# Six instead of four units start early in a seven-product gate/up stage, in pairs, with operand sums spread out

## The chip, the core and the metric

The kernel runs on one core of one Trainium2 chip. The metric is the device time of one execution in microseconds (us), median of several runs. Times inside a run come from a trace of one profiled execution; they count from the first instruction of that execution.

Names of engines: PE is TensorE (matmuls and transposes), DVE is VectorE, ACT is ScalarE, POOL is GpSimd, SP is SyncE, which issues the DMAs. PSUM is the memory that PE writes; this kernel divides it into eight banks of 128x512 fp32, five called `L` and three called `M`.

## The reference, cut to what matters

One decoder block over 1024 tokens of width 1024: an RMSNorm, an input projection, a state-space mixer beside a retention mixer, an output projection, and then the part that the change touches:

```
h = rmsnorm(x, norm2_w[i])
a = jax.nn.silu(jnp.einsum("bsd,df->bsf", h, w_gate[i]))
u = jnp.einsum("bsd,df->bsf", h, w_up[i])
x = x + jnp.einsum("bsf,fd->bsd", a * u, w_down[i])
```

followed by a last RMSNorm. D_FF is 2816, so `w_gate` and `w_up` are 1024x2816 each.

## The kernel before

**Numbers and halves.** Every fp32 operand of a large matmul is split into a high and a low part (`split`: ACT copies with rounding, DVE subtracts), and each product is three matmuls (high x high, high x low, low x high). The 1024 tokens are handled as two halves of 512, called h = 0 and h = 1.

**A list of steps sets the order.** `steps` is a list of (block, k). `run_all` walks it: it first prepares operands up to three steps ahead (`advance`: DMA issue, then `split`), then emits the matmuls of the step, then calls the functions hooked to that step with `at(i, f)`. PE runs in exactly this order. The other engines' orders come out of a scheduler that takes the code in this order with some priorities; on each engine instructions then run strictly one after the other.

**The gate/up stage.** It is computed with a 2x2x2 scheme of seven products instead of eight: weight columns in two halves of 128, the model dimension in two halves, tokens in two halves. A `Unit` is 256 columns of `w_gate` or `w_up`; there are 22, alternating gate and up. Each product of a unit is one step: 12 matmuls of 128x512. Products 1 and 2 need only the token half h = 0 (operands `B[1]`, `B[2]`, the normed and transposed half h = 0). Products 3 to 7 need sums of both halves. Products that start a sum take the PSUM banks by turns, five `L` banks, then three `M` banks. Product 2 adds into the PSUM bank of product 1, so between the two ACT must copy the result of product 1 out of that bank (line 166, into the tile `ktok`).

**What happens before the other products can run.** The token half h = 1 (tiles `x0` to `x3`) becomes final only at the end of the output projection. Then `scale` (lines 333 to 342) multiplies its four 128x1024 tiles by the norm's factors on DVE. For each of four k, `b_sums(k)` (lines 869 to 892) has PE transpose two 128x512 pieces into two `M` banks (a **lot** of eight transposes, line 163), and then DVE and ACT form the sums in place and split them: line 884 (ACT) and lines 886, 887, 890 (DVE), with splits at lines 195 (ACT) and 196 (DVE). The names in these instructions: `M` the two banks, called t2 and t1 in the code, `u` the scaled copy of t2, `m0` to `m15` the split operands, `h0` to `h2` and `S` the sums F. With three `M` banks, the second bank of a lot is the one that held t1 of the lot before, free once DVE has split t1 (line 196); the first bank held t2 of the lot before the last, free after line 890. `b_rest(k)` splits the two halves of F for products 7 and 4.

**Order at the start of the stage.** Four units run products 1 and 2 first, one unit after the other (eight steps), and the `b_sums` of the four k are hooked to the steps 2, 3, 4 and 5 of these, all `b_rest` to step 6. Then the same four units run products 6, 5, 7, 3, 4, and the other 18 units run all seven in the order 1, 6, 5, 2, 7, 3, 4. In the first part the weights come as single 256 KB loads; from product 6 of the first unit on, as two 512 KB tiles per unit into `x0`, `x1` or `x2`, `x3` (line 936), which become free when the last lot of transposes has read them. Operands of products lie in a ring of seven slots (`wp` three, `x4` to `x7`).

**After products.** `use` (lines 1003 to 1020) applies tanh (line 1010, ACT), multiplies (lines 1011 and 1019, DVE) and stores.

Of the kernel before, what the change touches and what calls it, by code (L numbers as in the profile page):

```python
# [9 lines left out]
F32 = mybir.dt.float32  # L10
F32R = mybir.dt.float32r
I32 = mybir.dt.int32
AF = mybir.ActivationFunctionType
ALU = mybir.AluOpType
# [3 lines left out]
P = 128  # L18
DM = 1024
SEQ = 1024  # L20
TH = 512
# [44 lines left out]
def block_kernel(ctx: ExitStack, tc: tile.TileContext, x, norm1_w, w_in, conv_w, conv_b,  # L66
# [12 lines left out]
    def T(shape, tag, dt=F32, bufs=1):  # L79
        uid[0] += 1  # L80
        return sb.tile(list(shape), dt, tag=tag, name=f"{tag}_{uid[0]}", bufs=bufs)

    def bank(tag):
        uid[0] += 1
        return psum.tile([P, 512], F32, tag=tag, name=f"{tag}_{uid[0]}", bufs={"L": 5, "M": 3}[tag])
# [4 lines left out]
    tt, stt, ts = nc.vector.tensor_tensor, nc.vector.scalar_tensor_tensor, nc.vector.tensor_scalar  # L90
    act = nc.scalar.activation
# [70 lines left out]
    def tr(o, a):  # L162
        tc.keep_in_program_order(nc.tensor.transpose(o, a, ident))  # L163
# [4 lines left out]
    def rsqrt(dst, src, scale, eps, n):  # L168

        w = T([P, 3, 16], "nw", bufs=3)  # L170
        v, t, i = w[:, 0, :n], w[:, 1, :n], w[:, 2, :n]
        ts(v, src, scale, eps, op0=ALU.mult, op1=ALU.add)
        ts(i.bitcast(I32), v.bitcast(I32), 1, None, op0=ALU.logical_shift_right)
        ts(dst.bitcast(I32), i.bitcast(I32), -1.0, 1597463007.0, op0=ALU.mult, op1=ALU.add)
        ts(v, v, -0.5, None, op0=ALU.mult)
        for _ in range(3):
            tt(t, dst, v, op=ALU.mult)
            tt(t, t, dst, op=ALU.mult)
            stt(dst, t, 1.5, dst, op0=ALU.add, op1=ALU.mult)
# [13 lines left out]
    def split(pair, src):  # L193

        a = act(pair[:, 0], src, AF.Copy).ins  # L195
        d = tt(pair[:, 1], src, pair[:, 0].bitcast(F32), op=ALU.subtract).ins  # L196
        return a, d
# [7 lines left out]
    steps = []  # L205
# [3 lines left out]
    def at(i, f):  # L209
        hooks.setdefault(i, []).append(f)  # L210
# [119 lines left out]
    def norm_pieces(get, wcol, tags, res, also=None):  # L330


        st = {}

        def scale():
            xt, ssq = get()
            rs = T([P, NT], "rs", bufs=2)
            tt(rs, ssq[:, :, 0], ssq[:, :, 1], op=ALU.add)
            rsqrt(rs, rs, 1.0 / DM, EPS, NT)
            for t in range(NT):  # L340
                ts(xt[t], xt[t], rs[:, t:t + 1], None, op0=ALU.mult)
            st["x"] = xt

        def one(k):
            def f():
                b = bank("M")
                for t in range(NT):
                    tr(b[:, t * P:(t + 1) * P], st["x"][t][:, k * P:(k + 1) * P])
                if also and k < 4:
                    if k == 0:  # L350
                        st["qk"] = T([P, 4, 2, TH], "qk", F32R)
                    hp = st["qk"][:, k]
                else:
                    hp = T([P, 2, TH], tags[k], F32R)
                w = cols[:, wcol + k:wcol + k + 1]
                act(hp[:, 0, :], b, AF.Copy, scale=w)
                stt(hp[:, 1, :], b, w, hp[:, 0, :].bitcast(F32), op0=ALU.mult, op1=ALU.subtract)
                res.append(hp)
                if also:
                    also(k)(b, w)  # L360
            return f
        return scale, [one(k) for k in range(8)]

    def load_x(h):
# [493 lines left out]

    B = {4: [], 7: [], "F": []}

    def b_first(k):

        def f(b, w):
            if k < 4:
                B["F"].append(T([P, 2, TH], f"h{k}" if k < 3 else "S"))
            act(B["F"][k % 4][:, k // 4, :], b, AF.Copy, scale=w)
        return f

    def b_sums(k):

        def f():
            if k == 0:
                for i in (5, 6, 7, 3):
                    o = {5: 0, 6: 4, 7: 8, 3: 12}[i]
                    B[i] = [T([P, 2, TH], f"m{q}", F32R) for q in range(o, o + 4)]
            bs = []
            for q in (k + 4, k):
                b = bank("M")
                for t in range(NT):
                    tr(b[:, t * P:(t + 1) * P], H[1]["x2"][t][:, q * P:(q + 1) * P])  # L880
                bs.append(b)
            t2, t1 = bs
            b22 = T([P, TH], "u", bufs=2)
            act(b22, bs[0], AF.Copy, scale=cols[:, 12 + k:13 + k])
            F = B["F"][k]
            stt(t1, bs[1], cols[:, 8 + k:9 + k], F[:, 0], op0=ALU.mult, op1=ALU.subtract)
            tt(t2, b22, t1, op=ALU.subtract)
            split(B[6][k], t2)
            split(B[5][k], t1)
            tt(F, F, t2.unsqueeze(1).to_broadcast([P, 2, TH]), op=ALU.subtract)  # L890
            split(B[3][k], b22)
        return f

    def b_rest(k):
        def f():
            split(B[7][k], B["F"][k][:, 0])
            B[4].append(T([P, 2, TH], f"h{(k + 3) % 4}", F32R))
            split(B[4][k], B["F"][k][:, 1])
        return f

    slots = [("wp", 3), ("x4", 1), ("wp", 3), ("x5", 1), ("wp", 3), ("x6", 1), ("x7", 1)]
    nslot = [0]
    units = [0]
    stage = {}

    def slot():
        tag, n = slots[nslot[0] % 7]
        nslot[0] += 1
        return T([P, 2, 4, P], tag, F32R, bufs=n)

    class Unit:
# [4 lines left out]

        def __init__(self, w, c0, st, use, prods=ORDER):
            self.w, self.c0, self.st, self.use, self.prods = w, c0, st, use, prods
            self.first = len(steps)
            steps.extend((self, k) for k in range(len(prods)))  # L920
            self.last = len(steps) - 1
            self.K = len(prods)
            self.op = {}

        def load(self, k):
# [58 lines left out]
    def gate_up():  # L984
        def temp():
            return T([P, TH], "wr", bufs=5)

        ss = []

        def c1(n):  # L990
            if n == 0:
                stage["c1"] = T([P, 4, TH], "ktok")
                b = T([P, 3, 4, P], "kcB")
                stage["s2"] = b[:, 2]
                stage["c15"] = b.rearrange("p k j q -> p k (j q)")
                a = T([P, 2, TH], "wb0")
                ss.extend((a[:, 0], a[:, 1]))
            return stage["c1"][:, n % 4]

        def pair_of(b):  # L1000
            def gate(q, ps, add):
                if len(ss) == 2 and q:
                    a = T([P, 2, TH], "S")
                    ss.extend((a[:, 0], a[:, 1]))
                g = ps
                if add is not None:
                    g = temp()
                    tt(g, ps, add, op=ALU.add)
                t = temp()
                act(t, g, AF.Tanh, scale=0.5)  # L1010
                stt(ss[q], t, 1.0, g, op0=ALU.add, op1=ALU.mult)

            def up(q, ps, add):
                u = ps
                if add is not None:
                    u = temp()
                    tt(u, ps, add, op=ALU.add)
                a = T([P, TH], "u", bufs=2)
                stt(a, u, 0.5, ss[q], op0=ALU.mult, op1=ALU.mult)  # L1019
                nc.sync.dma_start(aD[q % 2][2 * b + q // 2], a)  # L1020
            return gate, up

        class St(dict):
            def __missing__(self, k):
                assert k == "c1"
                self[k] = c1(self.n)
                return self[k]
        us, todo, n = [], [], 0
        for b in range(NF // 2):
            for w, use in zip((w_gate, w_up), pair_of(b)):  # L1030
                st = St()
                st.n = n
                n += 1
                todo.append((w, 256 * b, st, use))
        EARLY = 4
        us += [Unit(*a, (1, 2)) for a in todo[:EARLY]]
        us += [Unit(*a, (6, 5, 7, 3, 4)) for a in todo[:EARLY]]
        us += [Unit(*a) for a in todo[EARLY:]]
        return us

    def down_block(h, b):
        d = H[h]
# [79 lines left out]
    for h in range(2):  # L1122
        H[h]["O"] = list(out_blocks(h))
    GU = gate_up()
    for h in range(2):
        H[h]["D"] = [down_block(h, b) for b in range(2)]
# [81 lines left out]
    s0 = I0["z0"].first  # L1208
# [12 lines left out]
    scale, ks = norm_pieces(lambda: got["x"], 0, HT, H[1]["hT"])  # L1221
# [6 lines left out]
    scale, ks = [None] * 2, [None] * 2  # L1228
# [3 lines left out]
    s0 = H[1]["O"][0].first  # L1232
# [3 lines left out]

    def b_ready():
        B[1], B[2] = hT2[:4], hT2[4:]
    s0 = GU[0].first
    at(s0 - 1, b_ready)  # L1240
    at(s0 - 1, scale[1])
    for k in range(4):
        at(s0 + 2 + k, b_sums(k))
        at(s0 + 6, b_rest(k))

    def load_final():
        wbf.append(T([P, DM], "wb0"))
# [30 lines left out]
```

## Time and profile before

| | us |
|---|---|
| median of 3 runs | 1528.23 (1526.89 to 1529.42) |
| the profiled execution, its own time | 1528.46 |
| span of its trace, first to last instruction | 1526.7 |
| PE busy in the span | 1496.4 |
| DVE busy | 1018.6 |
| ACT busy | 625.2 |

The page gives, for each engine, busy time and share; 40 slices of the span with the busy share in tenths; the chain of work that ended last (here 92% PE); and groups of instructions by line with mean duration and the idle time in front of them. Matmuls are pipelined: one is listed with some 395 ns, but the next one starts after some 233 ns, so starts, not durations, tell the rate. The mean granted clock of TensorE over the span is 0.994 of full speed. Finer questions go to the trace: a list of who waited for whom, and a timeline of one engine in a stretch, where `[0.69 <-ACT ktok L166]` behind an entry says that the engine stood idle for 0.69 us before it and what ended that.

### The profile page before, as it was taken

What the parts mean: (1) busy time and instruction counts of PE and PEld (TensorE: products, weight loads), DVE (VectorE), ACT (ScalarE), POOL (GpSimd) and SP (SyncE); (2) the same over time, 40 slices, a digit from 0 to 9 for tenths busy, and PEclk for the clock granted to TensorE, in tenths of its full rate; (3) what the DMA queues carried; (4) which work ended last, traced back from release to release, by engine and by line L of the source; (5) the groups of instructions that cost most, each with busy time, mean ns of one, the idle gap of its engine ahead of it and who ended that gap; (6) DMA issues with size and microseconds to landing.
All of it is one profiled execution on the core that took longest, in us unless ns stands there. A gap on an engine that the chain in (4) does not pass through costs nothing.

```text
span 1526.7 us, 20790 instructions
## 1 busy us (share of the span) xinstructions
PE 1496.4 (98%) x7408; PEld 1222.3 (80%) x7408; DVE 1018.6 (67%) x2175; ACT 625.2 (41%) x1219; POOL 33.2 (2%) x67
## 2 busy tenths in 40 slices
PE   6999999999999999999999899999999999999997
PEld 5888878887889878878887688888888887788886
DVE  4587788767688896578746976666666665346345
ACT  5344457444354655333444522222222234344232
POOL 1011000000000000000000000000000000000000
PEclk8999999999999999999999999999999999999999
DMA  7433466473425567645533332222222238455331
GB/s 195 137 92 98 116 203 190 121 242 105 130 77 148 167 204 248 214 146 175 187 118 97 97 111 78 81 83 83 76 83 83 83 105 293 133 176 188 126 112 68
DMA packets 139369, 208.68 MB, mean 137 GB/s; under 512 B 11172, under 2 KB 69376, under 8 KB 139264
## 3 DMA queue, kind: packets, MB, share of 16 engines
q1 hardware_dynamic: 138096, 205.90, 43.6%
q0 software_dynamic: 432, 0.59, 0.6%
q8 instruction: 58, 0.95, 0.3%
q10 hardware_dynamic: 736, 0.86, 0.2%
q14 instruction: 47, 0.39, 0.1%
HBM read 166.34 MB, written 40.96 MB: 136 GB/s over the span
## 4 chain that ended last, share of the span: by engine, by line
PE 92%; DMA 4%; DVE 2%; ACT 1%; issue 1%; SPq 0%; ACTq 0%; DVEq 0%
PE L L160 74%; PE M L160 16%; PE M L163 2%; DMA m<-aD 1%; DMA wr<-in_w_in_dram 1%; DMA wr<-in_w_down_dram 1%; DVE m L196 0%; DMA x<-in_w_gate_dram 0%; DMA kc<-in_consts_dram 0%; DMA ktok<-aD 0%; ACT m L195 0%; DMA m<-mixD 0%; DVE wp L249 0%; DVE u L1019 0%; ACT wp L248 0%
## 5 line engine op out<-in xcount | busy, mean ns | idle before, releaser
L249 DVE TENSOR_TENSOR wp<-wr,wp 128x512 fp32r<-128x512 f32 (+2 forms) x328 | 217.7, 665 | 224.3 <-ACT wp L248 223.1
L160 PE MATMUL L<-wp,m 128*128 128x512 f32 x1512 | 357.3, 395 | 1.5 <-DVE wp L249 0.9
L248 ACT ACTIVATE wp<-wr 128x512 fp32r<-128x512 f32 (+2 forms) x328 | 199.6, 610 | 361.8 <-PE L L160 294.9
L160 PEld LDWEIGHTS L<-wp,m 128*128 128x128 f32 x1512 | 282.0, 188 | 68.7 <-DVE wp L249 2.4
L160 PE MATMUL L<-wp,h 128*128 128x512 f32 (+2 forms) x1248 | 260.0, 365 | 0.0
L160 PEld LDWEIGHTS L<-wp,h 128*128 128x128 f32 x1248 | 215.4, 188 | 30.6 <-issue 5.1
L160 PE MATMUL L<-h,wp 128*128 128x512 f32 x972 | 234.1, 398 | 0.7 <-ACT ktok L166 0.7
L160 PEld LDWEIGHTS L<-h,wp 128*128 128x128 f32 x972 | 180.6, 188 | 44.5 <-ACT ktok L166 1.1
L160 PE MATMUL L<-m,x 128*128 128x512 f32 x336 | 82.7, 395 | 1.6 <-ACT x L195 1.2
L160 PE MATMUL L<-h,x 128*128 128x512 f32 x336 | 83.3, 396 | 0.7 <-ACT ktok L166 0.7
L160 PE MATMUL L<-m,wp 128*128 128x512 f32 x312 | 77.1, 395 | 0.0
L160 PEld LDWEIGHTS L<-m,x 128*128 128x128 f32 x336 | 62.9, 188 | 17.2 <-ACT x L195 1.6
L160 PEld LDWEIGHTS L<-h,x 128*128 128x128 f32 x336 | 62.9, 188 | 16.3 <-ACT ktok L166 1.1
L160 PEld LDWEIGHTS L<-m,wp 128*128 128x128 f32 x312 | 58.5, 187 | 14.4
L195 ACT ACTIVATE wp<-wr 128x512 fp32r<-128x512 f32 x46 | 29.0, 630 | 66.6 <-DVE wr L948 57.5
L195 ACT ACTIVATE x<-x 128x512 fp32r<-128x512 f32 x40 | 24.9, 623 | 72.5 <-PE M L160 32.4
L389 DVE SCALAR_TENSOR_TENSOR m<-m,cols,m 128x512 f32<-128x512 f32 x72 | 52.1, 745 | 3.6 <-ACT m L387 3.4
L160 PE MATMUL M<-m,wp 128*128 128x512 f32 x216 | 53.4, 395 | 0.0
L160 PEld LDWEIGHTS M<-m,wp 128*128 128x128 f32 x216 | 40.5, 188 | 9.9
L160 PE MATMUL M<-m,x 128*128 128x512 f32 x192 | 47.1, 394 | 0.0
L196 DVE TENSOR_TENSOR m<-m 128x512 fp32r<-128x512 f32 x32 | 21.8, 690 | 35.5 <-ACT m L195 35.5
L160 PE MATMUL M<-h,x 128*128 128x512 f32 x180 | 44.5, 395 | 0.0
(280 smaller groups left out, 1952.4 us busy)
## 6 DMA issues: line engine op xcount, KB each, us to landing
wr<-in_w_in_dram SPq DMA_DIRECT2D x144, 256.0 KB, 2.8
wr<-in_w_down_dram SPq DMA_DIRECT2D x88, 256.0 KB, 2.9
wr<-in_w_out_dram SPq DMA_DIRECT2D x64, 256.0 KB, 2.9
aD<-u SPq DMA_DIRECT2D x44, 256.0 KB, 2.0
x<-in_w_gate_dram SPq DMA_DIRECT2D x22, 512.0 KB, 3.9
x<-in_w_up_dram SPq DMA_DIRECT2D x22, 512.0 KB, 3.9
x<-in_x_dram SPq DMA_DIRECT2D x16, 512.0 KB, 4.1
m<-rD SPq DMA_DIRECT2D x16, 512.0 KB, 4.1
```

The costliest lines, as they stand in the source:

```text
L160: tc.keep_in_program_order(nc.tensor.matmul(o, a, b, start=start, stop=stop, **kw))
L163: tc.keep_in_program_order(nc.tensor.transpose(o, a, ident))
L195: a = act(pair[:, 0], src, AF.Copy).ins
L196: d = tt(pair[:, 1], src, pair[:, 0].bitcast(F32), op=ALU.subtract).ins
L248: newest["act"] = act(pair[:, 0, :n], raw[:, :n], AF.Copy).ins
L249: newest["dve"] = tt(pair[:, 1, :n], raw[:, :n], pair[:, 0, :n].bitcast(F32), op=ALU.subtract).ins
L389: stt(dst, u[:, q:q + TH], w[q], dst, op0=ALU.mult, op1=ALU.add)
```

## The change

1. Six units instead of four run products 1 and 2 early, and they go in pairs: product 1 of both, then product 2 of both (12 steps). Six units then run 6, 5, 7, 3, 4; the other 16 run all seven.
2. `b_sums` is hooked to steps 2, 4, 6, 8 of the stage (before 2, 3, 4, 5), `b_rest` to steps 9 and 10 (before 6).
3. In `b_sums` the split of `b22` (operand of product 3) moves up: its ACT part right behind line 884, its DVE part ahead of the other splits.
4. The copies of product 1 need six places (before four); the two new ones take `x7`, so that the ring of operand slots has six slots.
5. `scale` of the second norm puts tiles 1 and 3 on ACT and leaves 0 and 2 on DVE, in both token halves.

```diff
             for t in range(NT):
-                ts(xt[t], xt[t], rs[:, t:t + 1], None, op0=ALU.mult)
+                if wcol and t % 2:
+                    act(xt[t], xt[t], AF.Copy, scale=rs[:, t:t + 1])
+                else:
+                    ts(xt[t], xt[t], rs[:, t:t + 1], None, op0=ALU.mult)
...
             act(b22, bs[0], AF.Copy, scale=cols[:, 12 + k:13 + k])
+            act(B[3][k][:, 0], b22, AF.Copy)
             F = B["F"][k]
             stt(t1, bs[1], cols[:, 8 + k:9 + k], F[:, 0], op0=ALU.mult, op1=ALU.subtract)
             tt(t2, b22, t1, op=ALU.subtract)
+            tt(B[3][k][:, 1], b22, B[3][k][:, 0].bitcast(F32), op=ALU.subtract)
             split(B[6][k], t2)
             split(B[5][k], t1)
             tt(F, F, t2.unsqueeze(1).to_broadcast([P, 2, TH]), op=ALU.subtract)
-            split(B[3][k], b22)
...
-    slots = [("wp", 3), ("x4", 1), ("wp", 3), ("x5", 1), ("wp", 3), ("x6", 1), ("x7", 1)]
+    slots = [("wp", 3), ("x4", 1), ("wp", 3), ("x5", 1), ("wp", 3), ("x6", 1)]
...
-                stage["c1"] = T([P, 4, TH], "ktok")
+                a, c = T([P, 4, TH], "ktok"), T([P, 2, TH], "x7")
+                stage["c1"] = [a[:, q] for q in range(4)] + [c[:, q] for q in range(2)]
...
-        EARLY = 4
-        us += [Unit(*a, (1, 2)) for a in todo[:EARLY]]
-        us += [Unit(*a, (6, 5, 7, 3, 4)) for a in todo[:EARLY]]
-        us += [Unit(*a) for a in todo[EARLY:]]
-        return us
+        EARLY = 6
+        first = len(steps)
+
+        for i in range(0, EARLY, 2):
+            us = [Unit(*a, (1, 2)) for a in todo[i:i + 2]]
+            steps.extend((u, k) for k in range(2) for u in us)
+        for i, a in enumerate(todo):
+            u = Unit(*a, (6, 5, 7, 3, 4) if i < EARLY else Unit.ORDER)
+            steps.extend((u, k) for k in range(len(u.prods)))
+        return first
...
-        at(s0 + 2 + k, b_sums(k))
-        at(s0 + 6, b_rest(k))
+        at(s0 + 2 + 2 * k, b_sums(k))
+        at(s0 + 9 + k // 2, b_rest(k))
```

What stands where, first on PE at the start of the stage. `L_1282` is the PSUM bank of the first unit, `qk` and `h4` to `h7` the token half h = 0 (for products 1 and 2), `wp`, `x4`, `x5` the weights' operands, `M_` lines the transposes. Before:

```order
L160 MATMUL L_1282_8078<-qk_1195_7545,wp_1271_8005 128x512 x12
L160 MATMUL L_1282_8078<-h4_1231_7752,x4_1273_8022 128x512 x3
L160 MATMUL L_1282_8078<-h5_1237_7799,x4_1273_8022 128x512 x3
L160 MATMUL L_1282_8078<-h6_1247_7846,x4_1273_8022 128x512 x3
L160 MATMUL L_1282_8078<-h7_1253_7893,x4_1273_8022 128x512 x3
L160 MATMUL L_1291_8120<-qk_1195_7545,wp_1281_8075 128x512 x12
L163 MATMUL M_1308_8150<-kc_1_63,x0_1146_7275 128x128
```

After:

```order
L160 MATMUL L_1282_8078<-qk_1195_7545,wp_1271_8005 128x512 x12
L160 MATMUL L_1289_8101<-qk_1195_7545,x4_1273_8022 128x512 x12
L160 MATMUL L_1282_8078<-h4_1231_7752,wp_1281_8075 128x512 x3
L160 MATMUL L_1282_8078<-h5_1237_7799,wp_1281_8075 128x512 x3
L160 MATMUL L_1282_8078<-h6_1247_7846,wp_1281_8075 128x512 x3
L160 MATMUL L_1282_8078<-h7_1253_7893,wp_1281_8075 128x512 x3
L163 MATMUL M_1309_8151<-kc_1_63,x0_1146_7275 128x128
```

Product 2 of the first unit stood right behind its product 1; now product 1 of the second unit (`L_1289`) lies between them.

Second, DVE between the split of t1 of the second lot (`m1`, first row) and that of the third lot (`m2`, last row), which frees the bank for the fourth lot of transposes. Before:

```order
L196 TENSOR_TENSOR m1_1293_8135<-M_1315_8196,m1_1293_8135 128x512
L890 TENSOR_TENSOR h1_1204_7599<-h1_1204_7599,M_1314_8191 128x1024
L886 SCALAR_TENSOR_TENSOR M_1322_8238<-M_1322_8238,cols_8_78,h2_1211_7648 128x512
L196 TENSOR_TENSOR m14_1306_8148<-u_1323_8243,m14_1306_8148 128x512
L887 TENSOR_TENSOR M_1321_8233<-u_1323_8243,M_1322_8238 128x512
L196 TENSOR_TENSOR m9_1301_8143<-h1_1204_7599,m9_1301_8143 128x512
L196 TENSOR_TENSOR h0_1333_8320<-h1_1204_7599,h0_1333_8320 128x512
L1011 SCALAR_TENSOR_TENSOR wb0_1285_8093<-wr_1325_8269,L_1320_8219 128x512
L196 TENSOR_TENSOR m6_1298_8140<-M_1321_8233,m6_1298_8140 128x512
L196 TENSOR_TENSOR m2_1294_8136<-M_1322_8238,m2_1294_8136 128x512
```

After:

```order
L196 TENSOR_TENSOR m1_1294_8136<-M_1319_8216,m1_1294_8136 128x512
L895 TENSOR_TENSOR h1_1204_7599<-h1_1204_7599,M_1318_8211 128x1024
L1012 SCALAR_TENSOR_TENSOR wb0_1286_8094<-wr_1326_8268,L_1317_8197 128x512
L890 SCALAR_TENSOR_TENSOR M_1328_8276<-M_1328_8276,cols_8_78,h2_1211_7648 128x512
L892 TENSOR_TENSOR m14_1307_8149<-u_1329_8281,m14_1307_8149 128x512
L196 TENSOR_TENSOR x6_1340_8354<-wr_1330_8292,x6_1340_8354 128x512
L1020 SCALAR_TENSOR_TENSOR u_1332_8309<-L_1323_8237,wb0_1286_8094 128x512
L891 TENSOR_TENSOR M_1327_8271<-u_1329_8281,M_1328_8276 128x512
L196 TENSOR_TENSOR m9_1302_8144<-h1_1204_7599,m9_1302_8144 128x512
L196 TENSOR_TENSOR h0_1343_8378<-h1_1204_7599,h0_1343_8378 128x512
L196 TENSOR_TENSOR m6_1299_8141<-M_1327_8271,m6_1299_8141 128x512
L196 TENSOR_TENSOR m2_1295_8137<-M_1328_8276,m2_1295_8137 128x512
```

Two more instructions stand in the interval than before: the split of an operand (`x6`) and line 1020, line 1019 of before.

## Rows read from the trace of the kernel before

**Rows 1.** Stretches: length; PE, weight loads, DVE, ACT, POOL busy; clock; DMA share, GB/s.

```profile
826.00:865.00 39.00, 30.83 (x143) 23.61 (x143) 35.94 (x66) 23.18 (x44) 0.00 (x0) 1.00 0.39 121
...
905.00:1270.00 365.00, 365.00 (x1567) 293.67 (x1567) 237.56 (x378) 109.92 (x192) 0.00 (x0) 1.00 0.29 91
```

**Rows 2.** Whom PE waited for, 800 to 1300 us: total, times, longest.

```profile
PE M L163 <- DVE m L196: 5.2, 3, 2.3
...
PE L L160 <- ACT x L195: 1.2, 1, 1.2
```

**Rows 3.** PE timeline at the start of gate/up: start, duration, what.

```profile
826.29 2.96 PE L160 MATMUL L<-qk,wp 128*128 128x512 f32 x12
829.94 3.05 PE L160 MATMUL L<-h,x 128*128 128x512 f32 x12 [0.69 <-ACT ktok L166]
832.83 2.96 PE L160 MATMUL L<-qk,wp 128*128 128x512 f32 x12
835.63 1.04 PE L163 MATMUL M<-kc,x 128*128 128x128 f32 x8
836.48 3.06 PE L160 MATMUL L<-h,x 128*128 128x512 f32 x12
...
841.36 0.63 PE L163 MATMUL M<-kc,x 128*128 128x128 f32 x4 [1.38 <-DVE m L196]
...
850.06 0.60 PE L163 MATMUL M<-kc,x 128*128 128x128 f32 x4
852.92 0.63 PE L163 MATMUL M<-kc,x 128*128 128x128 f32 x4 [2.26 <-DVE m L196]
853.31 3.01 PE L160 MATMUL L<-qk,x 128*128 128x512 f32 x12
857.00 3.06 PE L160 MATMUL L<-h,wp 128*128 128x512 f32 x12 [0.69 <-ACT ktok L166]
861.27 0.74 PE L160 MATMUL L<-m,x 128*128 128x512 f32 x2 [1.20 <-ACT x L195]
862.41 2.60 PE L160 MATMUL L<-m,x 128*128 128x512 f32 x10 [0.40 <-DVE x L196]
864.84 2.96 PE L160 MATMUL M<-m,wp 128*128 128x512 f32 x12
...
873.17 2.98 PE L160 MATMUL L<-h,x 128*128 128x512 f32 x12
```

**Rows 4.** DVE timeline of the same stretch.

```profile
831.45 2.74 DVE L341 TENSOR_SCALAR x<-x,rs 128x1024 f32<-128x1024 f32 x4
...
841.13 1.21 DVE L890 TENSOR_TENSOR h<-h,M 128x1024 f32<-128x1024 f32 x1
842.25 0.75 DVE L886 SCALAR_TENSOR_TENSOR M<-M,cols,h 128x512 f32<-128x512 f32 x1
842.92 0.68 DVE L196 TENSOR_TENSOR m<-u,m 128x512 fp32r<-128x512 f32 x1
843.51 0.69 DVE L887 TENSOR_TENSOR M<-u,M 128x512 f32<-128x512 f32 x1
...
858.65 0.69 DVE L948 TENSOR_TENSOR wr<-x,x 128x512 f32<-128x512 f32 x1 [0.49 <-DMA x<-in_w_gate_dram]
```

**Rows 5.** ACT timeline, three places of the stage.

```profile
829.29 0.60 ACT L166 ACTIVATE ktok<-L 128x512 f32<-128x512 f32 x1 [0.52 <-PE L L160]
833.03 0.60 ACT L1010 ACTIVATE wr<-L 128x512 f32<-128x512 f32 x1 [3.14 <-PE L L160]
...
1066.39 0.63 ACT L195 ACTIVATE x<-x 128x512 fp32r<-128x512 f32 x1 [6.66 <-PE L L160]
1073.36 0.63 ACT L195 ACTIVATE wp<-wr 128x512 fp32r<-128x512 f32 x1 [6.33 <-DVE wr L948]
```

**Rows 6.** SP timeline: issue of the first 512 KB weight loads.

```profile
853.29 0.92 SPq L936 DMA_DIRECT2D x<-in_w_gate_dram  x2
```

**Rows 7.** Group by line: shape and count, busy us, mean ns.

```profile
L631 ACT ACTIVATE m<-m 128x1024 f32<-128x1024 f32 x14 | 14.9, 1062 | 10.8 <-DMA m<-rD 6.0 <-PE M L160 4.8
```

More of the change, by code (lines that the diff above doesn't have):

```diff
@@ L906, in slot @@
     def slot():
-        tag, n = slots[nslot[0] % 7]
+        tag, n = slots[nslot[0] % len(slots)]
         nslot[0] += 1
@@ L918, in __init__ @@
             self.w, self.c0, self.st, self.use, self.prods = w, c0, st, use, prods
[L919 to L922, printed above, removed]
             self.op = {}
@@ L997, in c1 @@
                 ss.extend((a[:, 0], a[:, 1]))
-            return stage["c1"][:, n % 4]
+            return stage["c1"][n % 6]
         def pair_of(b):
@@ L1027, in __missing__ @@
                 return self[k]
-        us, todo, n = [], [], 0
+        todo, n = [], 0
         for b in range(NF // 2):
@@ L1238, in b_ready @@
         B[1], B[2] = hT2[:4], hT2[4:]
-    s0 = GU[0].first
+    s0 = GU
     at(s0 - 1, b_ready)
```

## The prediction

> **What bounds the kernel now.** Read first the busy time by stretch [rows 1]: from 905 to 1270 us PE is busy 365.00 of 365.00 us at full clock, so nothing that only relieves another engine there can help. From 826 to 865 us, where gate/up begins, PE is busy 30.83 of 39.00 us: 8.2 us idle. The list of waits [rows 2] says for whom: the second halves of three lots of transposes waited for DVE's split of t1, 5.2 us, and the first product 6 for an ACT split, 1.2 us. The PE timeline [rows 3] gives the rest. A product takes 2.80 us from start to start (832.83 to 835.63), a lot of eight transposes 0.85 (835.63 to 836.48). From 826.29 to 873.17, 46.88 us, PE ran 12 products and four lots, which is 12 x 2.80 + 4 x 0.85 = 37.0 us of work. So 9.9 us are lost: the 8.2 us of idle time and 1.7 us in which the matmul pipeline empties and fills around the seven gaps (the first gap is listed with 0.69 us, but 829.94 - 826.29 - 2.80 = 0.85).
>
> By cause: (a) product 2 right behind product 1, waiting for the copy out of the bank: 0.85 at 829.94 and 857.00 - 853.31 - 2.80 = 0.89 at 857.00, together 1.7. (b) The lots: 5.2 of idle and some 0.14 each to refill (the last one took 853.31 - 850.06 = 3.25 instead of 0.85), together 5.6. (c) The first product 6: 864.84 - 857.00 - 2 x 2.80 = 2.2. The remaining 0.3 or so is spread over products behind a gap; I leave it lost.
>
> **The pairs.** Between product 1 and 2 of a unit now lies another product. The copy starts right after PE's last matmul and takes 0.60 us [rows 5], under 2.80 us of cover. (a) goes to 0; without that cover it is 0.85 a time, as before. The total of products is the same, 22 x 7.
>
> **The scaling on two engines.** DVE did the four tiles from 831.45 in 2.74 us [rows 4], ready at 834.2. Now DVE has two (ready at about 833.5, since one operand split has moved into the computation of the factor and puts that 0.7 us later, to some 832.2). ACT has tile 1, then the copy of unit 2's product 1, then tile 3. The nearest row for a tile is an activation of the same shape, 1.06 us [rows 7]: 832.2 + 1.06 + 0.60 + 1.06 = 834.9. So the last tile comes 0.7 us later than before, not sooner. PE starts lot 1 at 826.29 + 3 x 2.80 = 834.7 and reads tile 3 with the fourth transpose, at 835.0. I take 0; the bounds are 0 and 0.5 us (one more copy ahead). DVE gains nothing by being free earlier: its next instruction needs the tanh of unit 1, which starts as PE ends product 2 (ACT's tanh begins where PE's product ended, 833.03, in rows 5), so DVE resumes at about 835.6.
>
> That ACT is the dearer engine here agrees with the Trainium skill (ScalarE: Activation LUTs, What ACT_TABLE_LOAD costs), which gives 186 ns + 0.833 ns per element and some 93 ns more for a per-partition scale: an estimate of 1.13 us a tile. By that tile 3 would be ready at 835.1, and the sum would rise by less than 0.1 us.
>
> The same edit in token half h = 0 puts two such tiles on ACT among operand splits of the output projection. These are made three products ahead, 8.4 us, so I take 0, with 0 to 1.1 us as bounds (one tile in front of a split that is just due).
>
> **The lots, spread over eight products.** This is the main term, and it is a race of DVE's queue against PE. DVE's pace from start to start [rows 4]: 0.60 us for a 128x512 instruction, 0.67 for line 886, 1.13 for line 890 (F). Follow the order of after from 835.6:
> - To the split of t1 of lot 1: ten instructions, 9 x 0.60 + 0.67 = 6.1, done at 841.7. PE is through lot 1 at 835.55, two products later at 841.15, and through the first half of lot 2 at 841.6. Wait: 0.15, with refill 0.3.
> - To t1 of lot 2: nine instructions, 1.13 + 0.67 + 7 x 0.60 = 6.0, done at 847.7. PE reaches the second half of lot 3 at 842.1 + 5.6 + 0.4 = 848.2. No wait, 0.5 to spare.
> - To t1 of lot 3: eleven instructions, two more than before the change's order had there (an operand split and line 1019), 1.13 + 0.67 + 9 x 0.60 = 7.2. One of them, the split of `x6`, needs its ACT half, the sixth ACT instruction counted from the tanh of unit 3, which can start at 848.0: 848.0 + 6 x 0.60 = 851.6, while DVE is there at 850.7. That adds 0.8. Done at 855.7. PE reaches the second half of lot 4 at 848.6 + 5.6 + 0.4 = 854.6. Wait 1.1, with refill 1.25.
> - The next product is the first of unit 6. Five units hold the five `L` banks, so it takes an `M` bank, that of t2 of lot 3, free after F: 855.7 + 1.2 = 856.9. PE is through lot 4 at 856.15. Wait 0.75, with refill 0.9. This wait is new: four units never needed an `M` bank.
>
> So (b) shrinks from 5.6 to about 2.4 us. Bounds: 0, if DVE keeps ahead, and 5.6, if it doesn't gain on PE at all.
>
> **The first product 6.** Its 512 KB weight tiles are issued as lot 4 has read `x0` to `x3`, and three products follow before it is due, where before there were two. Before: issue at 853.29 [rows 6], used by DVE at 858.65 [rows 4], 5.36 us. Now: issue at 856.15, there at 861.5. DVE then has three instructions (two of 0.60, F of 1.13, 863.9) and ACT splits the result behind two splits of F, to some 865.1. PE arrives at 857.0 + 3 x 2.80 = 865.4. So (c) goes from 2.2 to 0, but with only 0.3 us to spare; bounds 0 and 0.9 (one ACT and one DVE instruction more in front). The queue on SP: the store of unit 2 now stands ahead of the last single weight load and waits for line 1019 at 839.3; that load's split is due at 850.9, so 11 us hide it. POOL has no part.
>
> **Later.** Two more units run five products, with their first weights loaded twice (1 MB more in all; the DMA share there is 0.29 [rows 1]). DVE needs some 17 x 0.60 = 10.2 us in the 14.0 us of such a unit. I take 0.
>
> **Sum.** Lost before 9.9; after 0.3 + 0.3 + 1.25 + 0.9, rounded 2.4 with the scaling at 0 and the leftover 0.3 nearly within it, say 2.5. Gain 7.4. The profiled execution took 1528.46, 0.23 over the median of the three runs, which lie within 1.3 us of it: 1528.46 - 7.4 = 1521.1.
>
> **Rivals.** *Nothing is late any more* (DVE and ACT run a little faster in this order than their pace above): all 9.9 come back, 1518.6. Against it: the third interval has eleven instructions and a wait for ACT in 6.45 us of PE work.
>
> *DVE falls further behind.* DVE's queue and PE meet within 0.3 us at the first product 6, so each further microsecond that DVE stands waiting for an ACT half lands on PE. Three more waits like that of `x6`, 2.4 us, and the 0.9 at product 6 give 1521.1 + 3.3 = 1524.4; with the scaling's 0.5 and 1.1 as well, 1526.0. For it: ACT has more to do in this stretch. Against it: DVE was busy 35.94 of 39.00 us in this stretch [rows 1] with ACT halves in much the same order.
>
> *Slower: the ring of six.* ACT stands still until PE frees a slot: 6.66 us at 1066.39 [rows 5]. With one slot fewer it stands one product, 2.80 us, longer, and tanh and copies queue behind it. If that came through to PE once in each of the eight pairs of full units, it would cost 8 x 2.80 = 22.4, 1543.5. It decides from 7.4 / 8 = 0.93 us a pair. Against it: the instruction after that one waits 6.33 us for DVE anyway (1073.36, rows 5), more than the 2.80.
>
> That the scheduler undoes the change is excluded by the orders above.
>
> **How the numbers follow.** Forecast 0.74, nothing late 0.07, DVE further behind 0.15, ring 0.04. About 0.2%, 3.1 us, is what a measurement of this kernel can tell from no change, so DVE's rival is half faster and half same: faster 0.74 + 0.07 + 0.08 = 0.89, same 0.07, slower 0.04. The range reaches from the first rival, 1518.6, down a little for the runs' scatter, to the price of the second, 1524.4: 1518.2 to 1524.4. That leaves out the ring and the worse half of DVE's rival, and scatter.
>
> **What would show it.** In the profile after: no wait of line 160 for line 166; PE's waits for DVE at transposes down from 5.2 to about 1.3, nearly all at lot 4; a new wait of about 0.75 of a product in an `M` bank for F; the first product 6 without a wait, some 39 us after the first unit's start; PE without idle time behind it. Wrong would be: a wait at lot 1 for an ACT scaling over 0.5 us, waits at lots 2 or 3 over 0.5, product 6 late by over 1 us, or any PE wait between 905 and 1270.

## The result and the profile after

The changed kernel takes 1518.03 us (median of 6 runs, 1516.38 to 1518.63) against 1528.03 (6 runs, 1526.89 to 1529.42): ratio 0.9932, 95% interval 0.9919 to 0.9945, so 10 us faster. The forecast was 1521.1, its range 1518.2 to 1524.4: the direction and, in the gate/up stage, the mechanism were right, but the forecast gain was 2.6 us too small and the time lies 0.17 us under the range. The profiled execution took 1518.63, its span is 1516.8 us.

Windows of after, columns as in [rows 1]; the third row, 745 to 825 us, is the end of the output projection and comes up again below.

```profile
826.00:865.00 39.00, 37.52 (x177) 29.97 (x176) 34.46 (x64) 26.75 (x48) 0.00 (x0) 1.00 0.40 122
905.00:1270.00 365.00, 364.46 (x1567) 293.57 (x1566) 242.50 (x387) 113.08 (x193) 0.58 (x1) 1.00 0.30 97
745.00:825.00 80.00, 80.00 (x364) 65.18 (x363) 42.63 (x65) 34.83 (x60) 0.00 (x0) 1.00 0.36 114
```

PE was busy 30.83 of 39.00 us at the start of gate/up; now it is 37.52. The whole list of PE's waits from 800 to 1300 us (total, times, longest), against [rows 2]:

```profile
PE M L163 <- DVE m L196: 1.0, 1, 1.0
PE L L160 <- DVE wr L1018: 0.5, 1, 0.5
PE M L160 <- DVE h L895: 0.4, 1, 0.4
PE L L160 <- DVE wp L249: 0.3, 1, 0.3
PE L L160 <- ACT wp L248: 0.2, 1, 0.2
```

The waits for the copy (line 166) and for the first product 6 (line 195) are gone, and of 5.2 us at three lots 1.0 is left, at one lot. The last two rows belong to the down projection. The PE timeline of the stage, against [rows 3]:

```profile
825.14 2.97 PE L160 MATMUL L<-qk,wp 128*128 128x512 f32 x12
827.95 2.96 PE L160 MATMUL L<-qk,x 128*128 128x512 f32 x12
830.75 2.95 PE L160 MATMUL L<-h,wp 128*128 128x512 f32 x12
833.54 1.03 PE L163 MATMUL M<-kc,x 128*128 128x128 f32 x8
834.33 3.03 PE L160 MATMUL L<-h,x 128*128 128x512 f32 x12
837.20 2.96 PE L160 MATMUL L<-qk,wp 128*128 128x512 f32 x12
840.00 1.29 PE L163 MATMUL M<-kc,x 128*128 128x128 f32 x8
841.04 3.02 PE L160 MATMUL L<-qk,x 128*128 128x512 f32 x12
...
846.69 1.03 PE L163 MATMUL M<-kc,x 128*128 128x128 f32 x8
847.48 3.03 PE L160 MATMUL L<-h,x 128*128 128x512 f32 x12
...
853.15 0.60 PE L163 MATMUL M<-kc,x 128*128 128x128 f32 x4
854.76 0.63 PE L163 MATMUL M<-kc,x 128*128 128x128 f32 x4 [1.01 <-DVE m L196]
855.80 3.07 PE L160 MATMUL M<-qk,x 128*128 128x512 f32 x12 [0.41 <-DVE h L895]
858.71 2.96 PE L160 MATMUL L<-h,wp 128*128 128x512 f32 x12
```

Two products and one lot alternate; nothing stands between them until the second half of lot 4, and then the first product of unit 6, in an `M` bank, waits 0.41 us for F (line 895). Twelve products and four lots take 864.30 - 825.14 = 39.16 us (the thirteenth product, the first product 6, starts at 864.30) where before they took 46.88. This stretch is called the stage below.

Of DVE and ACT five rows matter (DVE's against [rows 4], ACT's against [rows 5] and [rows 7]):

```profile
850.33 0.69 DVE L196 TENSOR_TENSOR x<-wr,x 128x512 fp32r<-128x512 f32 x1 [0.83 <-ACT x L195]
853.34 1.28 DVE L196 TENSOR_TENSOR m<-M,m 128x512 fp32r<-128x512 f32 x2
860.52 0.69 DVE L948 TENSOR_TENSOR wr<-x,x 128x512 f32<-128x512 f32 x1 [0.52 <-DMA x<-in_w_gate_dram]
```

```profile
830.83 1.15 ACT L342 ACTIVATE x<-x,rs 128x1024 f32<-128x1024 f32 x1 [1.57 <-DVE rs L179]
832.37 1.14 ACT L342 ACTIVATE x<-x,rs 128x1024 f32<-128x1024 f32 x1
```

DVE waits 0.83 us for the ACT half of the `x6` split. Its splits of t2 and t1 of lot 3 (853.34) are done 0.14 us before PE's wait at lot 4 ends at 854.76. The weights of product 6 are issued at 855.10 and used at 860.52, 5.42 us later (5.36 before, [rows 4, 6]). ACT's scaled tile takes 1.15 us, not the 1.06 of the nearest row before.

### The profile page after: what moved, and what is told of

It is laid out like the page before. It is cut to its first block, busy times and chain, and to the rows that moved or that the text cites. A ratio compares the mean times of both kernels' runs of the same rounds, so it can differ in the third digit from the quotient of the medians.

```text
span 1516.8 us, 20817 instructions
## 1 busy us (share of the span) xinstructions
PE 1493.7 (98%) x7408; PEld 1222.5 (81%) x7408; DVE 1015.4 (67%) x2171; ACT 630.4 (42%) x1223; POOL 35.9 (2%) x67
## 4 chain that ended last, share of the span: by engine, by line
PE 95%; DMA 3%; ACT 1%; DVE 1%; issue 0%; SPq 0%; ACTq 0%
PE L L160 76%; PE M L160 17%; PE M L163 2%; DMA m<-aD 1%; DMA wr<-in_w_in_dram 1%; DMA wr<-in_w_down_dram 0%; DMA qk<-aD 0%; DMA kc<-in_consts_dram 0%; ACT m L195 0%; SPq L1058 0%; DVE wp L249 0%; ACT x L449 0%; DVE m L196 0%; ACT wp L248 0%; DVE u L1020 0%
## 5 line engine op out<-in xcount | busy, mean ns | idle before, releaser
L160 PE MATMUL L<-h,wp 128*128 128x512 f32 x1104 | 266.5, 397 | 0.0
L160 PEld LDWEIGHTS L<-h,wp 128*128 128x128 f32 x1104 | 205.4, 188 | 49.5 <-issue 1.0
L160 PEld LDWEIGHTS L<-wp,h 128*128 128x128 f32 x1248 | 215.3, 188 | 30.6 <-issue 5.1
L160 PE MATMUL L<-h,x 128*128 128x512 f32 x204 | 50.6, 396 | 0.5 <-DVE wr L1018 0.5
L1011 ACT ACTIVATE wr<-wr 128x512 f32<-128x512 f32 x33 | 20.9, 632 | 66.0 <-DVE wr L1009 64.9
L160 PEld LDWEIGHTS L<-h,x 128*128 128x128 f32 x204 | 38.1, 188 | 10.0 <-DVE wr L1018 1.0
L195 ACT ACTIVATE x<-x 128x512 fp32r<-128x512 f32 x27 | 17.0, 629 | 64.5 <-PE L L160 43.6
L160 PEld LDWEIGHTS M<-m,x 128*128 128x128 f32 x192 | 36.0, 188 | 8.6
```

The source lines that it names most:

```text
L160: tc.keep_in_program_order(nc.tensor.matmul(o, a, b, start=start, stop=stop, **kw))
```

## Where the ten microseconds are

Starts on PE cut the time up to its last matmul into five stretches: up to PE's 101st matmul or transpose, on to its 4001st (matmul 4000 in the expectations, which count from 0), to the first gate/up product, the stage, and the rest up to the last of all. Both kernels run 7408 of them, and the order is the same outside gate/up. In us, for three traces of before and two of after (e2, e11 and e1 are the two kernels repeated, see below):

| | to 101st | to 4001st | to gate/up | stage | rest |
|---|---|---|---|---|---|
| before | 35.70 | 685.65 | 104.95 | 46.88 | 644.70 |
| before, e2 | 36.02 | 685.78 | 105.09 | 47.02 | 642.66 |
| before, e11 | 35.31 | 686.03 | 104.84 | 46.96 | 643.96 |
| after | 35.09 | 685.70 | 104.35 | 39.16 | 643.32 |
| after, e1 | 35.14 | 685.78 | 104.35 | 39.15 | 643.35 |

Means differ by 7.8 in the stage, 0.6 in the third stretch, and 0.6, 0.1 and 0.4 in the others, 9.5 in all. The first column runs from 33.93 to 36.02 and the last from 641.79 to 645.04 over all thirteen traces of this study, whatever the kernel; in those two the difference is within what equal work scatters. So about 8.4 us belong to the change. From the start of the last matmul to the end of the span it is 8.8 us in the three traces of before and 9.2 in the two of after, so 0.4 us is lost again there, and the cause of that is open.

## The experiments

**e1_after_again and e2_before_again: the two kernels once more.** No edit.

> The changed kernel once more, for its trace. Of the 9.9 us between the two traces 7.8 lie in the stage (46.88 us before, 39.16 after, from the first unit's product 1 to the 13th product). Some 2 us lie elsewhere: 0.6 in the first 22 us, 0.5 at 743 to 747 us, and 0.9 net between the end of gate/up and the first steps of the down projection. Theory A, scatter of loads between executions: the stage again takes 39.1 to 39.3 us, but the parts outside move by 0.5 to 1.5 us against the first trace of the same kernel. Theory B, effects of the change: all parts agree with the first trace within 0.2 us, and so does the time, 1518.

> The kernel before once more, for its trace. Theory A (scatter): the stage takes 46.7 to 47.0 us again, while the first 22 us, 743 to 747 us and the stretch from the 13th product to the last matmul differ from the first trace by 0.5 us and more. Theory B (effects of the change): they agree within 0.2 us, with the same waits of PE at 745 us and at 1293 to 1304 us.

Measured: 1518.74 (5 runs, 1516.37 to 1519.12) against 1527.25 for before (15 runs), ratio 0.9936 [0.9924, 0.9949] (the quotient of the two medians is 0.9944); the one run of before for its trace took 1527.17. The stages repeat to 0.14 us (47.02 and 39.15). The two traces of after agree within 0.08 us in every stretch of the table, as theory B of e1 has it; those of before differ by 2.0 us in the last stretch, as theory A of e2 has it. Over all thirteen traces (above) that stretch scatters by 3.2 us, so the closeness of the two of after is partly luck. The wait of 0.54 us for line 1018 that the first trace of after has at 1258.96 is not in the second, where PE is busy 395.00 of 395.00 us from 875 to 1270.

**e3_no_scale: after, with DVE scaling all four tiles. e4_scale_only: before, with the shared scaling alone.** The edit, taken out in one and put in in the other:

```diff
             for t in range(NT):
-                ts(xt[t], xt[t], rs[:, t:t + 1], None, op0=ALU.mult)
+                if wcol and t % 2:
+                    act(xt[t], xt[t], AF.Copy, scale=rs[:, t:t + 1])
+                else:
+                    ts(xt[t], xt[t], rs[:, t:t + 1], None, op0=ALU.mult)
```

> The change without its scaling on two engines (all four tiles on DVE again, in both token halves). Theory A: the scaling is worth nothing in the stage, since the last tile comes later by it; the stage takes 39.1 to 39.3 us as with it, and the time is 1518 to 1518.5. Theory B: the 0.5 us at 743 to 747 us come from the scaling in token half h = 0, which frees DVE in front of an operand split of the output projection; then PE reaches the stage 0.5 us later than in the changed kernel, with the wait at 745 us back, and the time is 1518.5. Rival of both: the scaling in token half h = 1 feeds lot 1, and without it lot 1 waits 1 us or more: 1519 and over.

> The kernel before with nothing but the scaling on two engines. Theory A (worth nothing, or dearer at lot 1): the stage takes 46.9 to 47.6 us, since the last tile comes 0.7 us later and lot 1 has to wait for it, and the time is within 0.7 us of before. Theory B: the wait at 745 us is gone, 0.5 us. Together 1527.5 to 1528.5. Rival, that the scaling is part of the gain in the stage: under 46 us there.

Measured: e3 1518.38 (5 runs), ratio 0.9937 [0.9924, 0.9951]; e4 1527.31 (11 runs), ratio 1.0001 [0.9992, 1.0011]. The stage of e3 is 39.15 us, after's: in the stage the sharing is worth nothing, as forecast, and the rival, a wait at lot 1, falls. By the times alone it is worth nothing anywhere, but the third stretch says otherwise: 105.51 us in e3, 104.37 in e4. The waits of PE from 700 us to gate/up in e3:

```profile
PE L L160 <- DVE x L836: 0.9, 1, 0.9
PE M L163 <- DVE h L783: 0.2, 1, 0.2
```

In after and in e4 this list is empty, and the window from 745 to 825 us is busy for 80.00 of 80.00 us. In before, where the wait was shorter, the list is empty too, but the window has 79.89; the repeat e2 lists 0.4 us for line 836. The trace of e4 also holds something that no row of before had: its stage took 50.00 us and not the 46.9 to 47.6 expected, with waits that are together no longer than in before. Windows of 2 us in it, columns as in [rows 1] (the third figure from the end is the granted clock):

```profile
838.00:840.00 2.00, 0.67 (x5) 0.35 (x3) 2.00 (x5) 1.86 (x4) 0.00 (x0) 1.00 0.00 0
840.00:842.00 2.00, 1.39 (x6) 1.33 (x7) 1.94 (x3) 0.81 (x2) 0.00 (x0) 0.68 0.35 131
842.00:844.00 2.00, 2.00 (x7) 1.52 (x6) 2.00 (x4) 1.14 (x3) 0.00 (x0) 0.50 0.00 0
844.00:846.00 2.00, 2.00 (x11) 1.49 (x9) 1.40 (x3) 0.59 (x2) 0.00 (x0) 0.97 0.00 0
```

Behind a wait of 1.94 us at lot 2 the granted clock is 0.50 (the lower level, 1.2 GHz), and the next product takes 4.35 us instead of some 3.0. It happens once more behind the wait at lot 4 (2.26 us, product 4.59). Two such products are nearly all of the 3 us.

**e9_scale_h1 and e10_scale_h0_only: which token half it is.** After, with the sharing only for h = 1, and before, with it only for h = 0 (the list `res` is empty when the first half is scaled). The condition in e9, and with `not len(res)` in e10:

```diff
-                if wcol and t % 2:
+                if wcol and len(res) and t % 2:
```

> The kernel after, with the scaling shared by the two engines only for the second token half (at the gate/up stage); for the first half all four tiles are scaled by DVE, as before. Theory (the sharing pays in the first half, where DVE's scalings stand ahead of operand splits of the output projection): TensorE has idle time between 745 and 825 us, 0.1 to 1.4 us of it, as in all traces so far in which DVE scales alone; matmul 4000 to the first gate/up product 104.9 to 106.0 us; stage 39.2 us. Rival (the 0.6 to 1.6 us there are scatter of that stretch, not the scaling): as likely no idle time and 104.4 us.

> The kernel before, with the scaling shared by the two engines only for the first token half. Theory: TensorE is busy without idle time from 745 to 825 us, matmul 4000 to the first gate/up product 104.3 to 104.4 us, stage 46.9 to 47.1 us at full clock, or longer by 1.3 to 1.6 us for each product that falls into a stretch of half the clock behind a wait of 1.5 to 2.3 us. Rival (the sharing has nothing to do with it): idle time there of 0.1 to 1.4 us and 104.9 to 106.0 us.

Measured: third stretch 105.11 us in e9, 104.37 in e10, as the theory has it, and stages of 39.15 and 46.83; the times, of one run each, are 1518.51 and 1527.22. PE in e9:

```profile
744.50 5.80 PE L160 MATMUL L<-wp,m 128*128 128x512 f32 x24 [0.44 <-DVE x L839]
```

The wait is there, but just ahead of the window from 745 us that the expectation named, in which e9 is busy 80.00 of 80.00 us. Over all thirteen traces the third stretch is 104.84 to 105.98 us in the seven in which DVE scales the first half alone, and 104.35 to 104.37 in the six in which it is shared. The DVE rows of before and of after show why. Before:

```profile
742.12 0.75 DVE L341 TENSOR_SCALAR x<-x,rs 128x1024 f32<-128x1024 f32 x1
743.30 0.75 DVE L818 SCALAR_TENSOR_TENSOR m<-m,cols 128x512 fp32r<-128x512 f32 x1 [0.43 <-ACT m L817]
743.97 0.68 DVE L249 TENSOR_TENSOR wp<-wr,wp 128x512 fp32r<-128x512 f32 x1
744.57 2.72 DVE L836 SCALAR_TENSOR_TENSOR x<-L,rs,x 128x512 f32<-128x512 f32 x4
...
742.54 0.72 ACT L817 ACTIVATE m<-m,cols 128x512 fp32r<-128x512 f32 x1 [1.12 <-DMA m<-mixD]
```

After:

```profile
741.99 0.75 DVE L839 SCALAR_TENSOR_TENSOR x<-L,rs,x 128x512 f32<-128x512 f32 x1 [0.40 <-PE L L160]
742.66 0.68 DVE L249 TENSOR_TENSOR wp<-wr,wp 128x512 fp32r<-128x512 f32 x1
...
746.73 1.41 DVE L821 SCALAR_TENSOR_TENSOR m<-m,cols 128x512 fp32r<-128x512 f32 x2
```

In before the third of the four scalings and an operand's split (line 818) stand ahead of the residual additions (line 836, in after 839), which empty the `L` banks that PE needs next. That split waits for its ACT half (line 817), and this half for a load; the fourth scaling comes behind the additions, at 753.90. In after neither stands there, and the next of these splits (line 821) follows behind the additions. So DVE begins the additions 2.6 us earlier on the clock of the trace, 2.0 us against PE, whose 4001st matmul starts at 720.79 in after and at 721.35 in before. In the seven traces in which DVE scales the first half alone, its wait in front of that split is 0.43 to 1.56 us, and the additions begin 23.2 to 24.5 us after the 4001st matmul; in the other six they begin after 21.2 us. The gain of 0.5 to 1.6 us therefore varies with how late that load is. Whether it comes from the scaling that DVE is spared or from the new order of the split was not tried.

**e5_no_spread: after, with lots one product apart.**

```diff
-        at(s0 + 2 + 2 * k, b_sums(k))
-        at(s0 + 9 + k // 2, b_rest(k))
+        at(s0 + 2 + k, b_sums(k))
+        at(s0 + 6, b_rest(k))
```

> The kernel after, with the operand sums of the four lots at one product apart, as before (and their rests behind the last lot), pairs of products and scaling kept. Theory (a race of DVE's queue with PE): with one product, 2.8 us, of PE work between lots of about 6.5 us of DVE work, the second halves of lots 2 to 4 wait again for DVE's split of t1, together some 4 to 5 us with the refills, and the first product 6 still comes without a wait: stage (12 products and four lots) 43.5 to 45 us against 39.2 of after, time some 5 us above after, 1522 to 1524. Rival (two more units of cheap products ahead of product 6 do it alone, the spacing is not needed): stage within 1 us of after's 39.2 us, time 1517.5 to 1519.5.

Measured: 1524.24 (11 runs, 1522.83 to 1526.73), ratio 0.9982 [0.9974, 0.9991], so 5.5 to 6.2 us above after; stage 45.79. Its PE waits from 820 to 880 us, one row in all:

```profile
PE M L163 <- DVE m L196: 6.6, 3, 2.9
```

This is the theory's picture: lots 2 to 4 wait again, product 6 does not, and the rival falls. The stage is 0.8 us longer than was expected; the trace has one product at the lower clock behind the first of these waits (4.32 us from 840.74), which is 1.3 us of it.

**e6_no_pairs: after, with product 2 right behind product 1.**

```diff
-            steps.extend((u, k) for k in range(2) for u in us)
+            steps.extend((u, k) for u in us for k in range(2))
```

> The kernel after, with product 2 of each of the six units right behind its product 1 again, all else kept. Theory: the copy of product 1 out of its bank waits on PE's end and is waited for by product 2, so PE loses 0.85 to 0.9 us where DVE's lots do not hold PE up anyhow; of six places two or three show it: stage 41 to 42 us, time 1519.8 to 1521. Rival (the copy was hidden behind other waits all along, the pairs bring nothing): stage 39.2 to 39.8, time 1517.5 to 1519.

Measured: 1519.72 (5 runs, 1519.41 to 1522.25), ratio 0.9958 [0.9945, 0.9970]; stage 41.67, 2.5 above after. Its PE waits from 820 to 880 us:

```profile
PE M L163 <- DVE m L196: 1.1, 2, 0.8
PE M L160 <- DVE u L1020: 0.9, 1, 0.9
PE L L160 <- ACT ktok L166: 0.7, 1, 0.7
PE M L160 <- ACT x L166: 0.7, 1, 0.7
```

Of six units two, the first and the last, have no lot between their products, and they wait for the copy, 0.69 us each, as in [rows 3]. The first product 6 comes later and has to wait for a bank (line 1020). The time is 0.1 us under the expected stretch, the stage within it, and the rival falls.

**e7_pairs_only: before, with its four units in pairs.** The same edit the other way round, with four units, a ring of seven and lots one product apart.

> The kernel before, with its four half-alone units taken in pairs (product 1 of two units, then product 2 of both), nothing else changed: four units, ring of seven, lots one product apart, scaling on DVE. Theory: the two waits of line 160 for the copy (0.85 and 0.89 us) go, but DVE's queue is as long as before, so the waits at the lots or at the first product 6 grow by a part of it: stage 45.3 to 46.3 us against 46.9 to 47.0 of before, time 0.7 to 1.6 us below before. Rival A (waits are independent, the sum of the parts holds): stage 45.2 or less, 1.7 us below before. Rival B (all of it is given back at the lots): stage 46.6 to 47.2, time as before.

Measured: 1527.84 (11 runs), ratio 1.0003 [0.9993, 1.0013]; stage 46.94. Its waits:

```profile
PE M L163 <- DVE m L196: 4.8, 3, 1.6
PE L L160 <- ACT x L195: 2.1, 1, 2.1
PE L L160 <- DVE x L196: 0.4, 1, 0.4
```

```profile
861.35 4.14 PE L160 MATMUL L<-m,x 128*128 128x512 f32 x10 [0.37 <-DVE x L196]
```

The copies are waited for no more (-1.7 with refill), the lots a little less, the first product 6 0.9 us more: idle time falls from 8.2 to 7.3 us. Then the ten matmuls behind that wait, 2.60 us in [rows 3], take 4.14 at a lower clock. At full clock the stage would be 45.4, inside the theory's stretch. The time shows no gain, as rival B had it; in this trace that is a lower clock, not the lots, but one trace cannot say that it is so in all eleven runs.

**e8_ring6: before, with six slots.**

```diff
-    slots = [("wp", 3), ("x4", 1), ("wp", 3), ("x5", 1), ("wp", 3), ("x6", 1), ("x7", 1)]
+    slots = [("wp", 3), ("x4", 1), ("wp", 3), ("x5", 1), ("wp", 3), ("x6", 1)]
```

> The kernel before, with the ring of weight slots six deep instead of seven, nothing else changed. Theory: ACT stands idle at a slot for several us and DVE's half is later than ACT's, so the shorter ring costs PE nothing: stage 46.9 to 47.1 and the rest of gate/up 397.0 to 397.6 us, as before; time within 0.1% of before. Rival (the ring's wait comes through to PE in each pair of units): the rest of gate/up over 398.5 us, up to 420, time slower by that.

Measured: 1526.90 (11 runs), ratio 1.0001 [0.9992, 1.0010]; rest of gate/up 396.57 us (397.28 to 397.50 in before): the ring costs nothing there, and the rival falls. The changed kernel, with its own ring of six, has 397.55 and 397.10 us there. ACT's wait for a slot did grow, from the 6.66 us of [rows 5] to

```profile
1073.00 0.63 ACT L195 ACTIVATE x<-x 128x512 fp32r<-128x512 f32 x1 [7.68 <-PE L L160]
```

and the instruction behind it now waits 3.49 us for DVE instead of 6.33. In this trace the stage was 49.26 us: the first product 6 waited 2.30 us (its load was used 6.49 us after issue, not 5.36) and then ran at a lower clock. The median does not show it.

**e11_before_third: before once more, for its clock.** No edit.

> The kernel before once more, for its stage. Theory (waits of 1.5 to 2.3 us at the lots are sometimes followed by a stretch at half the clock, which the two traces of before so far did not show): stage 46.9 to 47.1 us at granted clock 1.00, or some 48.3 or 49.7 with a clock of 0.83 to 0.97 in it; idle time between 745 and 825 us, and 104.9 to 106.0 us from matmul 4000 to the first gate/up product. Rival (the half clock belongs to the edited kernels): 46.9 to 47.1 us.

Measured: 1527.67; stage 46.96 at granted clock 1.00, third stretch 104.84. None of three traces of before has the lower clock in the stage, and four of the five edited kernels that have long waits there do (e4, e5, e7, e8; not e10). e4 has before's order of products and lots in the stage, and the wait of 2.26 us at lot 4, behind which its clock fell, is before's to 0.01 us; so that wait by itself does not decide it, and with so few traces it stays open what does.

## Where the prediction was right and where it failed

*(a) The copies.* This was right: there is no wait for line 166. e6 shows what the cover is worth, 2.5 us of stage with all that follows from it.

*(b) The lots.* This was right in kind: what is left of the waits is nearly all at lot 4, 1.01 us against 1.1. The wait for F is 0.41 instead of 0.75. Lot 2 takes 841.04 - 840.00 = 1.04 us, 0.2 over a free lot (forecast 0.15 and refill); lot 3 nothing. The wait of DVE for the `x6` split is 0.83, forecast 0.8. e5 shows that the spacing is what brings this about.

*(c) The first product 6.* This was right: it does not wait. ACT's half (line 195, at 863.44 for 0.61) is there 0.25 us ahead of PE, forecast 0.3.

*First failed step: the sum.* The race, followed step by step, put the end of PE's wait for F at 856.9, 30.6 us after the start of the stage, and the first product 6 at 865.4, 39.1 us after it. Measured are 855.80 - 825.14 = 30.66 and 39.16. Against 46.88 that alone is a gain of 7.8. The sum instead added a refill to each wait, and a leftover. But the wait for F ends when DVE is done, so what PE loses in refills ahead of it only makes that wait shorter: it was reckoned as 0.75 and took 0.41. The sum's terms add up to 2.75 us as they stand, and it set them at 2.5; 39.16 - 37.0, some 2.2 us, are lost. The gain came out as 7.4, 0.4 too small.

*Second failed step: the scaling in half h = 0.* It was taken as 0 with 0 to 1.1 us of cost as bounds, from ACT's side alone. DVE's side was not read: there a scaling, and an operand's split that waits for a load, stand ahead of the additions that free PE's banks. By e3, e4, e9 and e10 the output projection is 0.5 to 1.6 us shorter with the sharing, so the bound had the wrong sign. At lot 1 the 0 was right, though the term in it was not: a tile takes 1.15 us. The Trainium skill's estimate (ScalarE: Activation LUTs, What ACT_TABLE_LOAD costs) was 1.13 us, nearer than the row of another line.

*Third failed step: the range.* Its lower end was the first rival, 1518.6, less 0.4 for scatter, on the base of one execution of 1528.46. Before's median is 1528.03 in the runs of the result and 1527.2 in the later ones, and equal work at the start and in the rest differs by 2 to 3 us between executions. From 1527.2, the 7.8 and 0.6 shown, less the 0.4 behind the last matmul, give 1519.2; the medians of after are 1518.0 and 1518.7. So on which side of 1518.2 a median falls is scatter, and the second one lies inside the range. Of the 3.1 us by which the forecast is too high the base accounts for 0.4, the sum for 0.4 and the scaling for 0.6; the remaining 1.7 or so no run assigns to the change.

*The rivals.* "Nothing late any more" gave nearly the time, but by luck: of the 9.9 us that it took back the stage gave 7.8, with 1.4 us of waits left in it, the output projection gave 0.6, and the rest is within scatter. DVE did not fall further behind, and the ring costs nothing (e8). One of the signs of being wrong came up: a PE wait between 905 and 1270, 0.54 us, in one of two traces.

*Open.* The spacing was not tried with four units, whose eight products leave no room for it. What six units bring without it shows only in e5 against e7, 6.6 us of idle time against 7.3. Part 3 of the change was in no run taken out by itself; in before the DVE split of `b22` already stands ahead of line 887 for lot 2 [rows 4], so little is to be expected of it, but that is not shown. How often the lower clock comes up in before, and so whether closing the gaps gains more than the idle time, is not settled either: there are 3 traces without it, against a spread of its times of 1525.39 to 1531.35 (27 runs) and of 1516.37 to 1519.12 for after (5 runs).

## What to carry to other kernels

Where PE meets an in-order engine several times in a row, follow both queues from one start to one end and take the gain from the two arrival times; a sum of waits, refills and leftovers can count some of them twice, as it did here. When work moves from one engine to another, price both sides at every place where it happens: what the receiving engine delays, and what stood behind that work in the queue of the one relieved. Give parts that lean on each other (pairs and spacing) a price together: pairs alone brought no measurable time here, and without them the whole loses 2.5 us of its stage.

## What the runs showed of the hardware that was not expected

A wait of about 2 us on PE can be followed by a product at half the clock: four traces (e4, e5, e7, e8) had granted clocks down to 0.50 behind waits of 1.9 to 2.9 us, each worth 1.2 to 1.6 us more, while before in three traces, and e10, have waits of 2.26 us at clock 1.00, and after, whose longest wait in the stage is 1.01, has none of it. The same 512 KB loads were used 5.36 us after issue in one trace, 5.42 in another and 6.49 in a third.
